# Splitting the weights of a two-layer decoder trunk: the low halves on one engine, in one instruction a unit

## The chip, the cores and the metric

The kernel runs on one core of a Trainium2 chip. The metric is the time of one execution on the device in microseconds (us), the median of three. Engines are named as in the profile: PE is TensorE (matrix products), PEld its weight loads, DVE is VectorE, ACT is ScalarE, POOL is GpSimd, SP is SyncE, which issues the DMAs. The products with the weights take fp32r operands, each split into a high and a low part.

## What is computed

Two layers of a decoder on 256 tokens of width 1024, each of them a token mixer, a cross-attention into 256 memory tokens and a SwiGLU feed-forward block (FFN), all added to the residual stream.

```python
# layer 0: combined projection, sparse attention A beside block attention B, one output projection
aq, ak, av, iq, ik, iw, bq, bk, bv = split(rms_norm(x) @ ab_w_in)
x += concat(dsa(aq, ak, av, iq, ik, iw), moba(bq, bk, bv)) @ ab_w_out
# layer 1: compressed, selected and window branches, mixed by gates
q, kc, vc, ks, vs, kw, vw, gt = split(rms_norm(x) @ nsa_w_in)
x += nsa(q, rope(q), compress(kc), compress(vc), ks, vs, kw, vw, sigmoid(gt)) @ nsa_w_out
# both layers
x += attention(rms_norm(x) @ w_q, rms_norm(mem) @ w_kv) @ w_o
g, u = split(rms_norm(x) @ ffn_w_in);  x += (silu(g) * u) @ ffn_w_out
```

## The kernel before

**The weight stream.** All weights pass through once as 232 units of two blocks of 128 rows and up to 512 columns (512 KB). A unit lands by DMA in one of three places named raw. `pusher` (line 384) makes its high part (`move`, ACT or DVE, one instruction on 128x1024) and then its low part, raw minus high, in two instructions, one for each block of rows (`tt`, line 313: DVE or POOL). Both parts lie in one of six places named whl. Then the raw place is free and the DMA of the unit three further on is issued. PE reads a unit for both tiles of 128 tokens: for each block the products high*high, high*low and low*high (`mm3`), twelve in all, most of them 512 columns wide.

**The order.** Nobody writes the order out by hand. Each piece of work is a generator that yields instructions; `Steps.run` (line 107) takes, again and again, the one that can start first by a rough clock (`Est`, line 140: a time for each engine, and for each tile's last write and reads). An instruction that two engines can do (`either`) goes to the one that is done with it first (`Op.best`, line 66); DVE has to be ahead by 0.4 us for that. So the costs written in `Est.Engine.cost` settle which engine does what and how instructions stand in each engine's queue. On the chip each engine works through its queue in that order; semaphores make it wait for operands.

**The work beside the stream.** Each projection's result is taken out of PSUM by DVE or ACT, normed, rotated (`rope`, four instructions on DVE or POOL), scaled, split and transposed by PE. Attention: scores (PE, tile sp), mask and maximum (DVE, sn<-sp), exponential (ACT), reciprocal (DVE), scaling (`scale`: sn<-sn,rc, DVE or POOL), transposes (PE, DVE or ACT to pt), values (PE, po). POOL alone makes the roots (`pow_half`, e.g. rq<-hss). In the FFN, DVE multiplies each result of u with silu(g) (t<-mm), PE transposes it, and DVE and ACT split it (slab<-tp).

**Main** (line 1468) walks through mixer, memory keys (mk), output projection (out), memory attention (mq, mv, mo) and FFN of each layer. `mixer1` ends with the projections q0 and q1; `mem_prep(1)`, which loads the memory tokens, transposes and splits them, is spawned ahead of these two, at line 1224. Its tiles are read by the products mk.

Of the kernel before, what the change touches and what calls it, by code (L numbers as in the profile page):

```python
# [8 lines left out]
F32 = mybir.dt.float32  # L9
# [6 lines left out]
P = 128  # L16
# [41 lines left out]
class Op:  # L58
    """an instruction to be issued, on the one of its engines that is done with it first"""
# [6 lines left out]
    def best(self):  # L66
        """(end, start, way)"""
        if self.deps is None:
            self.deps = [self.est.after(e, outs, ins) for e, outs, ins, _, _ in self.ways]
        r = []  # L70
        for d, w in zip(self.deps, self.ways):
            t = max(d, self.est.clk[w[0]])
            r.append((t + w[3], t, w))
        return min(r, key=lambda q: q[0] + (SHY if q[2][0] == "V" else 0.0))
# [9 lines left out]
class Steps:  # L84
    """The order of issue: pieces of work as generators, which yield instructions and conditions to wait for. Of the
    instructions that an engine could start next, one of the lowest rank goes first."""
# [9 lines left out]
    def go(self, th):  # L96
        """th up to its next instruction or to a condition that isn't met"""
# [42 lines left out]
class Est:  # L140
    """A rough clock of every engine and of every tile's last write, to emit work about when its operands are there."""

    def __init__(self, nc):
        self.clk = {"PE": 0.0, "V": 0.0, "S": 0.0, "G": 0.0, "D": 0.0}
# [11 lines left out]
    def when(self, ap, tab, e="", raw=True):  # L156
        """when engine e can go on after the uses of ap in tab; raw: it reads what they wrote"""
# [7 lines left out]
    def follow(self, old, new):  # L165
        """a new tile in the place of an old one is written after the old one's last use"""
# [18 lines left out]

    def issue(self, e, outs, ins, cost):
        t = max(self.clk[e], self.after(e, outs, ins))
# [9 lines left out]
        self.clk[e] = t  # L197
        for a in ins:
            self.note(a, self.rd, t, e)
# [52 lines left out]
class Slots:  # L252
    """n places of one size; a tile is placed in a free one"""
# [5 lines left out]
    def idle(self, i):  # L259
        """when the last use of place i ends"""  # L260
        return self.est.end(self.last[i]) if i in self.last else 0.0
# [22 lines left out]
def trunk(ctx: ExitStack, tc: tile.TileContext, I, out):  # L284
# [17 lines left out]
    def move(o, i, scale=None):  # L302
        """o = i * scale"""
# [4 lines left out]
    def together(ops):  # L308
        """ops one right after the other"""
# [3 lines left out]
    def tt(o, a, b, op):  # L313
        """o = a op b, all in SBUF"""
        return either(V.tensor_tensor(o, a, b, op=op), PO.tensor_tensor(o, a, b, op=op))

    def scale(s, r, n, m):
        """s [P, n*m] times r [P, n], in place"""
# [20 lines left out]
    # ---------------------------------------------------------------- loads of the small things  # L339
# [10 lines left out]
    # ---------------------------------------------------------------- weight stream  # L350
# [33 lines left out]
    def pusher():  # L384
        for i in range(len(plan)):
# [5 lines left out]
            for j in range(2):  # L391
                yield tt(u.lo[:, j], raw[:, j, :n], u.hi[:, j].bitcast(F32), OP.subtract)
# [37 lines left out]
    # ---------------------------------------------------------------- constants  # L430
# [34 lines left out]
    # masks of scores of the wrong sign: +1e30 where a key is not to be seen  # L465
# [10 lines left out]
    def tables():  # L476
# [24 lines left out]
        # products of the gains of queries and keys: dsa, moba, sel, win (these of the wrong sign), cmp, mem 0, mem 1  # L501
# [36 lines left out]
    def rope(q, H, a, b, half):  # L538
        """in place on the first 2*half dims of q [P, H, *]; a, b [P, 2, half]"""
# [9 lines left out]
    # ---------------------------------------------------------------- products with the weights  # L549
# [11 lines left out]
    def gemm(key, t, h, K, ev, need=None, part=None):  # L561
        """a pass of tile t: h(k) -> (hi, lo) [P, P], of which need tells; ev(psum, free, t) goes on with the result;
        part: the columns, where it isn't all"""
# [18 lines left out]
    # ---------------------------------------------------------------- norms and transposes  # L582
# [6 lines left out]
    def ms_root(ss, n, L, t):  # L589
        """mean square + eps and its root's inverse"""  # L590
# [7 lines left out]
    def evac_gain(ps, free, hi, lo, gain):  # L598
        """hi, lo [P, 4, P] of the product of ps with the gains [P, 4] of its blocks"""
# [9 lines left out]
    def norm(key, t, col, ver):  # L609
        """hT[t] from x[t], once both halves of x[t] are at version ver"""  # L610
# [14 lines left out]
    def root(key, t):  # L625
        """mean square + eps of the norm and its root's inverse"""
# [11 lines left out]
    def inv_rms(ps, H, dh, v, mul, add_k, r):  # L638
        """r [P, H] = (sumsq * mul + add_k * eps * v)^-0.5 of the heads of ps [P, H*dh]"""
# [10 lines left out]
    def stack_T(q, dst):  # L650
        """dst(i) [P, 4, P] of 4 heads: rows 0-63 hi, rows 64-127 lo, of the transposed heads of q [P, 8, HD]"""
# [12 lines left out]
    def keys_T(src, n, dst, gain):  # L664
        """dst(i) = (hi, lo) [P, P], both halves alike, of the transposed src(i) [P, 128] (a head twice) times gain;
        dst takes pairs at once"""
# [14 lines left out]
    # ---------------------------------------------------------------- softmax attention  # L681
    def scores(t, sp, spf, items, mask, gate, sn, snf, pv, fin):
        """items: (columns of sp, r) - softmax of the negated scores sp times r, times gate; pv(p) adds its transposed
        blocks p times the values"""
# [40 lines left out]
    def split(ps, free, hi, lo):  # L725
        """hi, lo of ps"""
# [4 lines left out]
    def finish(po, pof, t, half):  # L731
        """the transposed parts of the heads' outputs po for the output projection"""
# [6 lines left out]
    # ---------------------------------------------------------------- layer 0 mixer  # L739
# [203 lines left out]
    # ---------------------------------------------------------------- layer 1 mixer  # L943
# [19 lines left out]
    def mixer1():  # L963
# [30 lines left out]
        def compress():  # L994
# [40 lines left out]
            # the values of 8 heads, one below the other, each in its own columns  # L1035
# [490 lines left out]
```

## Time and profile before

| | us |
|---|---|
| runs: median (lowest to highest of 3) | 823.25 (822.81 to 828.13) |
| the profiled execution: span of its records | 824.0 |
| PE busy in it | 773.2 (94%) |
| DVE busy | 529.9 (64%) |
| POOL busy | 450.1 (55%) |
| ACT busy | 423.5 (51%) |

Busy is the time in which an instruction of the engine is on record as running, so an instruction that has started and is held up inside counts as busy. Idle time of an engine is put down to what ended it. In rows, whl<-raw,whl is a low part, whl<-raw a high part, and mm<-whl,h a product with the weights.

### The profile page before, as it was taken

To read this page: it belongs to the slowest core of one execution; us is meant where nothing else is said; L and a number is where in the kernel's file an instruction comes from. 1 tells how busy PE (TensorE), PEld (TensorE's weight loads), DVE (VectorE), ACT (ScalarE), POOL (GpSimd) and SP (SyncE) were. 2 spreads that over 40 slices of the span, in tenths; PEclk is the share of its full clock that TensorE was granted. 3 is DMA by queue.
4 is the path that set the end of the run, shared out by engine and by line. 5 is a ranking of instruction groups with operands and counts; after the bars stand their busy time and mean duration, and the time that the engine had idled before them with its cause. 6 is when DMAs were issued, how large, how long until landed. Compare 5 with 4: busy or idle time off the path is not lost.

```text
span 824.0 us, 12365 instructions
## 1 busy us (share of the span) xinstructions
PE 773.2 (94%) x4259; PEld 632.2 (77%) x4259; DVE 529.9 (64%) x1175; ACT 423.5 (51%) x799; POOL 450.1 (55%) x362
## 2 busy tenths in 40 slices
PE   5888999999999999999898988999999999999998
PEld 3676777797877878887677776778797778879886
DVE  6999998776655554322628889896867654454222
ACT  4566765465534433434425757665666344434441
POOL 4668844536555544667427765433536555545662
PEclk9899999999999999999999999999999999999999
DMA  6634423645565564886524732123535655645661
GB/s 188 179 103 112 155 92 103 180 127 154 153 181 160 176 187 115 214 228 205 152 64 124 219 112 78 45 61 103 151 99 160 202 162 160 191 140 164 209 206 73
DMA packets 69486, 121.31 MB, mean 147 GB/s; under 512 B 8420, under 2 KB 15664, under 8 KB 69424
## 3 DMA queue, kind: packets, MB, share of 16 engines
q1 hardware_dynamic: 69392, 120.53, 48.9%
q8 instruction: 33, 0.54, 0.3%
q14 instruction: 29, 0.24, 0.1%
q0 software_dynamic: 32, 0.00, 0.0%
HBM read 119.46 MB, written 1.05 MB: 146 GB/s over the span
## 4 chain that ended last, share of the span: by engine, by line
PE 56%; DVE 23%; DMA 7%; issue 6%; ACT 4%; POOL 3%; SPq 1%; ACTq 0%; DVEq 0%; POOLq 0%
PE mm L221 41%; PE po L221 8%; DVE whl L221 7%; PE tp L221 5%; DMA raw<-in_ffn_w_out 4%; ACT whl L221 3%; DVE t L221 3%; DVE sn L221 2%; POOL whl L221 2%; PE sp L221 2%; DVE slab L221 2%; DVE acc L221 2%; DMA raw<-in_ffn_w_in 2%; DMA raw<-in_nsa_w_in 1%; DVE x L221 1%
## 5 line engine op out<-in xcount | busy, mean ns | idle before, releaser
L221 POOL TENSOR_TENSOR whl<-raw,whl 128x512 fp32r<-128x512 f32 (+3 forms) x225 | 346.5, 1549 | 248.2 <-ACT whl L221 191.3
L221 PE MATMUL mm<-whl,h 128*128 128x512 f32 (+3 forms) x1776 | 403.7, 381 | 3.3 <-DVE whl L221 2.3
L221 PEld LDWEIGHTS mm<-whl,h 128*128 128x128 f32 x1776 | 311.8, 190 | 61.0 <-issue 2.8
L221 DVE TENSOR_TENSOR whl<-raw,whl 128x512 fp32r<-128x512 f32 (+3 forms) x239 | 216.2, 914 | 174.0 <-ACT whl L221 173.1
L221 ACT ACTIVATE whl<-raw 128x1024 fp32r<-128x1024 f32 (+3 forms) x203 | 204.8, 1011 | 182.4 <-DMA raw<-in_ffn_w_out 61.7
L221 PE MATMUL mm<-whl,slab 128*128 128x512 f32 (+1 forms) x840 | 201.4, 377 | 1.1 <-DVE x L221 1.1
L221 PEld LDWEIGHTS mm<-whl,slab 128*128 128x128 f32 x840 | 141.5, 189 | 27.4 <-issue 2.2
L221 PE MATMUL po<-whl,slab 128*128 128x512 f32 x264 | 68.4, 397 | 0.0
L221 PEld LDWEIGHTS po<-whl,slab 128*128 128x128 f32 x264 | 49.9, 190 | 11.9
L221 ACT ACTIVATE slab<-tp 128x256 fp32r<-128x256 f32 (+2 forms) x64 | 28.9, 472 | 47.2 <-PE tp L221 44.9
L221 ACT ACTIVATE sn<-sn,mx 128x128 f32<-128x128 f32 (+1 forms) x96 | 42.7, 447 | 10.1 <-DVE mx L221 9.3
L221 PE MATMUL tp<-ident,t 128*128 128x128 f32 x224 | 35.3, 278 | 10.7 <-DVE t L221 10.0
L221 PEld LDWEIGHTS tp<-ident,t 128*128 128x128 f32 x224 | 26.3, 142 | 21.3 <-DVE t L221 12.5
L221 POOL TENSOR_TENSOR sn<-sn,rc 128x512 f32<-128x512 f32 (+2 forms) x25 | 23.3, 932 | 34.4 <-DVE rc L221 19.4
L221 PE MATMUL tp<-ident,sn 128*128 128x128 f32 (+1 forms) x180 | 30.2, 280 | 6.3 <-DVE sn L221 2.9
L221 DVE CUSTOM_DVE_ANT_0 sn<-sp,cm,rq 128x128 f32<-128x128 f32 (+1 forms) x80 | 30.7, 407 | 5.8 <-PE sp L221 5.8
L221 ACT ACTIVATE pt<-tp 128x512 f32<-128x512 f32 (+2 forms) x49 | 25.8, 534 | 16.6 <-PE tp L221 15.8
L221 DVE CAST whl<-raw 128x1024 fp32r<-128x1024 f32 (+2 forms) x29 | 23.1, 795 | 15.3 <-PE mm L221 13.1
L221 DVE TENSOR_TENSOR x<-mm,x 128x512 f32<-128x512 f32 x36 | 24.5, 685 | 13.0 <-PE mm L221 13.0
L221 ACT ACTIVATE t<-mm,rh 128x512 f32<-128x512 f32 (+1 forms) x26 | 17.0, 655 | 30.4 <-PE mm L221 30.4
L221 PEld LDWEIGHTS tp<-ident,sn 128*128 128x128 f32 (+1 forms) x180 | 20.4, 140 | 14.2 <-issue 5.1
L221 ACT ACTIVATE h<-gv 128x512 fp32r<-128x512 f32 x20 | 12.6, 632 | 33.7 <-DVE gv L221 33.7
(208 smaller groups left out, 711.7 us busy)
## 6 DMA issues: line engine op xcount, KB each, us to landing
raw<-in_ffn_w_in SPq DMA_DIRECT2D x80, 512.0 KB, 4.3
raw<-in_ffn_w_out SPq DMA_DIRECT2D x44, 512.0 KB, 4.6
raw<-in_ab_w_in SPq DMA_DIRECT2D x16, 512.0 KB, 3.6
raw<-in_mem_w_kv SPq DMA_DIRECT2D x16, 512.0 KB, 3.7
raw<-in_nsa_w_in SPq DMA_DIRECT2D x16, 512.0 KB, 4.1
raw<-in_ab_w_out SPq DMA_DIRECT2D x8, 512.0 KB, 3.7
raw<-in_mem_w_q SPq DMA_DIRECT2D x8, 512.0 KB, 3.7
raw<-in_mem_w_o SPq DMA_DIRECT2D x8, 512.0 KB, 4.4
```

The costliest lines, as they stand in the source:

```text
L221: return f(*a, **{q: v() if q in ("start", "stop") and callable(v) else v for q, v in k.items()})
```

## The change

Four things are changed. The low part of a unit is one instruction on 128x1024, on DVE alone. `Est` gets one more clock, "port", which DVE instructions with two tensor inputs outside PSUM and all POOL instructions share: each starts, by the rough clock, not before the other's last one has ended. `Op.best` counts it when it picks the engine. And `mem_prep(1)` is spawned after q0 and q1, behind a new condition at which main stops until all queries of layer 1 have been prepared. Comments and blank lines, which the change removes too, are left out here.

```diff
@@ Op.best
-            t = max(d, self.est.clk[w[0]])
+            t = max(d, self.est.clk[w[0]], self.est.clk["port"] if self.est.locks(w[0], w[1], w[2]) else 0.0)
@@ Est
-        self.clk = {"PE": 0.0, "V": 0.0, "S": 0.0, "G": 0.0, "D": 0.0}
+        self.clk = {"PE": 0.0, "V": 0.0, "S": 0.0, "G": 0.0, "D": 0.0, "port": 0.0}
...
+    @staticmethod
+    def locks(e, outs, ins):
+
+        if e == "V":
+            big = [a for a in ins if a.shape[1:] != [1] and tuple(a.shape[1:]) != (1,)]
+            return len(big) > 1 and not any("PSUM" in str(a.space) for a in (*big, *outs))
+        return e == "G"
+
     def issue(self, e, outs, ins, cost):
-        t = max(self.clk[e], self.after(e, outs, ins))
+        lock = self.locks(e, outs, ins)
+        t = max(self.clk[e], self.after(e, outs, ins), self.clk["port"] if lock else 0.0)
...
+        if lock:
+            self.clk["port"] = t
@@ pusher
-            for j in range(2):
-                yield tt(u.lo[:, j], raw[:, j, :n], u.hi[:, j].bitcast(F32), OP.subtract)
+            yield V.tensor_tensor(u.lo, raw[:, :, :n], u.hi.bitcast(F32), op=OP.subtract)
@@ mixer1
-        spawn(mem_prep(1), 2)
         yield from both((1, "q0"), h, KD, ev_q(0))
         yield from both((1, "q1"), h, KD, ev_q(1))
+        yield lambda: len(qrT) == 2 * G and len(quT) == 2 * NT
+        spawn(mem_prep(1), 2)
```

What this does to the queues is seen at three places.

The first is POOL's queue at the start of the program. whl are the low parts, h the split of the normed input, rh and rk roots. Before:

```order
L221 TENSOR_TENSOR whl_120<-raw_79,whl_120 128x424
L221 TENSOR_TENSOR whl_162<-raw_81,whl_162 128x424
L221 TENSOR_TENSOR h_112<-gv_157,h_111 128x512
L221 TENSOR_TENSOR whl_174<-raw_85,whl_174 128x424
L221 TENSOR_TENSOR rh_190<-vh_189,mhalf 128x1
L221 TENSOR_TENSOR whl_217<-raw_160,whl_217 128x424
L221 TENSOR_TENSOR whl_240<-raw_172,whl_240 128x512
```

With the change, POOL's queue at the same place:

```order
L232 TENSOR_TENSOR rh_186<-vh_185,mhalf 128x1
L232 TENSOR_TENSOR rh_248<-vh_247,mhalf 128x1
L232 TENSOR_TENSOR rk<-ssk,mhalf 128x1 x2
L232 AFFINE_SELECT cm<-cm 128x128
L232 AFFINE_SELECT cmn<-cmn 128x30
L232 TENSOR_TENSOR rope_411<-t_241,ia 128x64
L232 TENSOR_TENSOR rope_411<-t_241,ib 128x8x4 x2
```

No low part is left on POOL (225 instructions in the whole program); the rope instructions, most of which DVE had, are there instead. POOL has 197 instructions in all, 367 before; DVE 1082, before 1161; ACT 671, before 654; PE has the same 3969.

The second is DVE's queue in the FFN of layer 0, between the products u of the two tiles: t<-mm takes such a result out of PSUM, slab<-tp splits the transposed one. Before:

```order
L221 SCALAR_TENSOR_TENSOR t_2628<-mm_2668,rh_2410,t_2628 128x512
L221 CAST whl_2722<-raw_2659 128x1024
L221 TENSOR_TENSOR slab_2709<-tp_2712,slab_2708 128x2x128
L221 TENSOR_TENSOR slab_2711<-tp_2712,slab_2710 128x2x128
L221 TENSOR_TENSOR whl_2722<-raw_2659,whl_2722 128x512
L221 TENSOR_TENSOR whl_2739<-raw_2673,whl_2739 128x512
L221 TENSOR_TENSOR whl_2751<-raw_2695,whl_2751 128x512
L221 SCALAR_TENSOR_TENSOR t_2669<-mm_2705,rh_2443,t_2669 128x512
```

With the change:

```order
L232 SCALAR_TENSOR_TENSOR t_2570<-mm_2608,rh_2359,t_2570 128x512
L232 CAST whl_2660<-raw_2599 128x1024
L232 TENSOR_TENSOR slab_2647<-tp_2650,slab_2646 128x2x128
L232 TENSOR_TENSOR slab_2649<-tp_2650,slab_2648 128x2x128
L232 TENSOR_TENSOR whl_2660<-raw_2599,whl_2660 128x1024
L232 TENSOR_TENSOR whl_2676<-raw_2612,whl_2676 128x1024
L232 TENSOR_TENSOR whl_2687<-raw_2632,whl_2687 128x1024
L232 SCALAR_TENSOR_TENSOR t_2609<-mm_2643,rh_2402,t_2609 128x512
```

The queue keeps its shape; the three low halves in it become three whole low parts.

The third is PE's queue in layer 1, at the end of the last product of q1 (mm<-whl,h). The products mk read a slab; tp, sp and po are attention's. Before:

```order
L221 MATMUL mm_4766<-whl_4593,h_113 128x512 x2
L221 MATMUL mm_4766<-whl_4593,h_114 128x512
L221 MATMUL mm_4998<-whl_4627,slab_4568 128x512
L221 MATMUL tp_4984<-ident,sn_4839 128x128 x4
L221 MATMUL tp_4994<-identr,t_4977 128x128 x4
L221 MATMUL mm_4998<-whl_4627,slab_4568 128x512
```

With the change:

```order
L232 MATMUL mm_4524<-whl_4459,h_113 128x512 x2
L232 MATMUL mm_4524<-whl_4459,h_114 128x512
L232 MATMUL tp_4661<-ident,sn_4565 128x128 x4
L232 MATMUL sp_4612<-slab_4144,slab_4556 128x256
L232 MATMUL sp_4612<-slab_4148,slab_4556 128x256
```

Before, the products mk follow at once and are mixed with attention's; with the change the next 80 rows of the queue are attention's alone, and mk begins behind them.

## Rows read from the trace of the kernel before

**Rows 1.** The page, part 1: busy time, share of span, instructions; PE, PEld.

```profile
PE 773.2 (94%) x4259; PEld 632.2 (77%) x4259; DVE 529.9 (64%) x1175; ACT 423.5 (51%) x799; POOL 450.1 (55%) x362
```

**Rows 2.** Busy time by stretch: start:end and length, then busy (instructions) by engine.

```profile
core 0: us, PE busy (x) PEld busy (x) DVE busy (x) ACT busy (x) POOL busy (x), PEclk, DMA share, GB/s
0.00:140.00 140.00, 118.06 (x651) 92.10 (x652) 126.89 (x380) 87.98 (x196) 89.49 (x91) 0.98 0.45 137
360.00:380.00 20.00, 20.00 (x88) 16.02 (x87) 6.28 (x9) 8.80 (x9) 14.69 (x9) 1.00 0.67 209
480.00:560.00 80.00, 75.26 (x604) 60.77 (x603) 73.70 (x269) 58.09 (x186) 34.86 (x40) 1.00 0.19 62
```

**Rows 3.** Groups by shape, low halves: busy us, mean ns | idle before.

```profile
L221 POOL TENSOR_TENSOR whl<-raw,whl 128x512 fp32r<-128x512 f32 x202 | 323.3, 1609 | 215.7 <-ACT whl L221 173.6 <-DVE whl L221 25.8 <-issue 4.7
...
L221 DVE TENSOR_TENSOR whl<-raw,whl 128x512 fp32r<-128x512 f32 x206 | 196.5, 963 | 162.7 <-ACT whl L221 161.9
```

**Rows 4.** Timeline at 24 us, POOL and DVE: start, us, engine, instruction.

```profile
23.75 3.05 POOL L221 TENSOR_TENSOR whl<-raw,whl 128x512 fp32r<-128x512 f32 x2 [0.16 <-ACT whl L221]
...
24.50 1.08 DVE L221 COPY ia<-cos 128x8 f32<-128x8 f32 x1
25.49 0.16 DVE L221 COPY ib<-nsin 128x8 f32<-128x8 f32 x1
25.57 1.27 DVE L221 COPY ia<-cos 128x8 f32<-128x8 f32 x1
```

**Rows 5.** Groups by shape: DVE splits with one input in PSUM; rope.

```profile
L221 DVE TENSOR_TENSOR slab<-tp,slab 128x256 fp32r<-128x256 f32 x44 | 17.4, 418 | 6.5 <-ACT slab L221 6.5
...
L221 DVE TENSOR_TENSOR slab<-tp,slab 128x512 fp32r<-128x512 f32 x4 | 2.7, 684 | 0.0
...
L221 DVE TENSOR_TENSOR rope<-t,rb 128x64 f32<-128x64 f32 x15 | 2.9, 212 | 0.0
```

**Rows 6.** Timeline of DVE: the two scalings on 128x1024 in SBUF.

```profile
61.31 2.31 DVE L221 TENSOR_TENSOR t<-t,rk 128x1024 f32<-128x1024 f32 x1
...
73.97 1.29 DVE L221 TENSOR_TENSOR t<-t,rk 128x1024 f32<-128x1024 f32 x1
```

**Rows 7.** Timeline of DVE: first and last held instruction of mixer 0.

```profile
9.09 1.49 DVE L221 TENSOR_TENSOR whl<-raw,whl 128x424 fp32r<-128x424 f32 x1
...
130.45 1.78 DVE L221 TENSOR_TENSOR sn<-sn,rc 128x512 f32<-128x512 f32 x1
```

**Rows 8.** Timeline of DVE: first and last held one of attention in layer 1.

```profile
495.11 1.08 DVE L221 TENSOR_TENSOR rope<-t,ra 128x128 f32<-128x128 f32 x1
...
562.17 1.77 DVE L221 TENSOR_TENSOR whl<-raw,whl 128x512 fp32r<-128x512 f32 x1
```

**Rows 9.** Timeline of PE: last values of attention 0 and 1, last product out.

```profile
134.04 0.66 PE L221 MATMUL po<-pt,bv 128*64 128x128 f32 x8
...
565.55 0.66 PE L221 MATMUL po<-pt,vv 128*64 128x128 f32 x8
...
579.76 1.64 PE L221 MATMUL mm<-whl,slab 128*128 128x512 f32 x6
```

**Rows 10.** Timeline of the FFN, from 249 us, and PE's last such wait.

```profile
249.01 4.80 DVE L221 TENSOR_TENSOR whl<-raw,whl 128x512 fp32r<-128x512 f32 x3
...
250.57 1.06 ACT L221 ACTIVATE whl<-raw 128x1024 fp32r<-128x1024 f32 x1 [0.39 <-DMA raw<-in_ffn_w_in]
253.74 0.74 DVE L221 SCALAR_TENSOR_TENSOR t<-mm,rh,t 128x512 f32<-128x512 f32 x1
...
254.53 0.66 PE L221 MATMUL tp<-ident,t 128*128 128x128 f32 x4 [1.15 <-DVE t L221]
...
725.23 0.66 PE L221 MATMUL tp<-ident,t 128*128 128x128 f32 x4 [1.15 <-DVE t L221]
```

**Rows 11.** Timeline at 89 us: a root on POOL, and DVE meanwhile.

```profile
88.92 0.68 DVE L221 TENSOR_TENSOR whl<-raw,whl 128x512 fp32r<-128x512 f32 x1
88.96 2.43 POOL L221 TENSOR_TENSOR rq<-hss,mhalf 128x8 f32<-128x8 f32 x1
...
90.68 0.67 DVE L221 CAST whl<-raw 128x1024 fp32r<-128x1024 f32 x1
```

## The prediction

> **What bounds the kernel now.** I read the page's busy times first, then the table by stretch, then the groups by shape, then timelines. PE is busy 94% [rows 1], which looks like a kernel with nothing to give. The table by stretch says otherwise. In the FFN, at 360 to 380 us, PE is busy all the time and gets 88 products through, 0.227 us each; DVE is busy a third of it [rows 2]. There PE is the bound. In mixer 0 (0 to 140 us) and attention of layer 1 (480 to 560 us) DVE is busy 126.9 of 140 and 73.7 of 80 us, and PE's instructions there, many of them small, stand further apart than their size needs [rows 2]. In these two stretches the end is set by DVE.
>
> But DVE's busy time is not all work. At 24 us two copies of 8 columns take 1.08 and 1.27 us, and one of the same size between them 0.16; the long ones end when POOL's two low halves end (23.75 + 3.05 = 26.80, against 25.57 + 1.27 = 26.84) [rows 4]. DVE stands still inside an instruction while POOL works in SBUF. The low halves show it from both sides: 0.963 us on DVE, 1.609 on POOL [rows 3], where a split of that width that has an input in PSUM takes 0.684 [rows 5].
>
> The Trainium skill (Perfetto Trace Analysis, Identifying the Most-Contended Engine) says that occupancy is a fair measure for VectorE of how near it is to its limit. Here the copies contradict it: seven eighths of their occupancy is standing still. By the page the mixers have no room for more work on DVE, and the sum would be that of the second rival below, 836; by the rows it is the one that follows.
>
> **The price of a whole low part.** From 256 to 512 columns a split goes from 0.418 to 0.684 us [rows 5], 1.04 ns a column, so 1024 columns take 0.684 + 512 x 0.00104 = 1.22 us. The bounds are the two scalings on 128x1024 from SBUF, 1.29 us and, held by POOL, 2.31 [rows 6]. I take 1.22, since POOL's low parts, which hold most, are gone.
>
> **Mixer 0.** I went through DVE's timeline to 134 us, where the last values of attention 0 are read [rows 9], and compared each instruction with the shortest of its form: 21 are held by a low half on POOL by over 0.3 us, 18.6 us in all [rows 7]. That goes. What comes is in the order: up to DVE's last score of this attention, 22 low halves at 0.69 (15.2 us) become 28 whole low parts at 1.22 (34.2), so +19.0. What leaves DVE up to there, mostly 36 pieces of rope (like the one at 0.21 us [rows 5]), three high parts and three copies of pt, comes to 9.6 us at the undisturbed duration of each form. Sum for DVE: -18.6 + 19.0 - 9.6 = -9. Attention ends 9 us sooner, and the order has 336 of the 384 weight products up to the end of out behind it by then, 296 before: 40 x 0.23 = 9 us less for PE to do afterwards. If PE had the room, mixer 0 would end 18 us sooner; but it must then be much denser than before, and the first 20 us wait for loads. Bounds 0 and -18; I take **-10**, the DVE sum and a little.
>
> **Layer 1, mixer.** From 480 us to the end of attention at 566 [rows 9] only five instructions are held by low halves, 4.7 us [rows 8]; the scalings of sn, which stay on POOL, hold about as much. Between the first and the last score DVE's own work falls by 3.4 us (order, undisturbed durations: fewer rope pieces, casts and splits of the memory, which come later, against 7 whole low parts for 10 halves). So attention gets shorter by some 8 us. The moved `mem_prep(1)` takes part of it back. It issues two loads on SP later, and main waits at the new condition for all queries; behind main wait mk and out. PE has 119 weight products inside attention before and 90 now, and 69 instead of 56 left at its end: 13 x 0.23 = +3.0 us. Ahead of 480 us the stretch is a chain of norms and projections, in which DVE is held some 9 us by low halves; I count -1 for it, since DVE is seldom what is late there. Sum **-6**; bounds +3 (nothing gained but the tail paid) and -12.
>
> **FFN.** The queue keeps its shape. At 249 us DVE needs 4.80 us for three low halves, and t<-mm behind them starts at 253.74; PE's transposes wait 1.15 us for it [rows 10]. Now: the first whole part from 249.1 to 250.3, the second to 251.5, the third after its high part on ACT (250.57 + 1.06 = 251.63) from 251.75 to 252.97. So t<-mm starts 0.77 us sooner, and 0.4 us of PE's wait stay. There are five of these in both FFNs, the last at 725 us [rows 10]: 5 x 0.77 = **-4**. Bounds: -5.7, or +2 if the third part is held by something. Everywhere else in the FFN, PE is full and hides what happens to DVE and POOL: a unit lasts PE 12 x 0.23 = 2.8 us, DVE 1.22.
>
> **At nothing.** The eight more high parts on ACT (1.06 us each [rows 10]) lie under PE, as ACT is half idle [rows 1]. Rope on POOL is slower for its own chain, but POOL loses 225 low halves of its 450 us. The raw places come free about 0.5 us sooner; PE waits hardly ever for a unit, so this gives nothing. The norms between blocks (140 to 220 and 560 to 640 us) are chains in which a held DVE instruction and a longer low part weigh about the same: 0, bounds 2 either way.
>
> **Sum.** -10 - 6 - 4 = -20 on a span of 824.0: 804.0. The median of the runs is 0.75 under the span, so **803** us.
>
> **Rivals.** *PE is the bound after all.* It is busy 94% [rows 1]; what DVE saves it spends waiting for PE, and only the FFN's waits go: 824.0 - 4 - 0.75 = 819. For it: 75.3 of 80 us of PE in attention are busy [rows 2]. Against it: there are 7.5 instructions a microsecond in that stretch, most of them on 64 to 256 columns, and a product of 512 columns alone takes 0.227. The Trainium skill (same page and section) calls matmul busy time a bad measure and weight loads a good one; by these, attention at 60.8 of 80 (76%) is nearly as full as the FFN at 16.0 of 20 (80%) [rows 2], which would speak for this rival. I hold against it that a load for a transpose takes as long as one for 512 columns, so that the share says little here. Chance 0.20.
>
> *DVE's busy time is work.* The waits do not go but change sides: a low part of 1.22 us meets POOL's scalings and ropes with twice the length. The clock "port" that should keep them apart is off in two ways: it leaves out instructions with one input, which are held too [rows 4], and counts the roots, during which DVE ran a low half in 0.68 and a high part in 0.67 us [rows 11]. Then mixer 0 grows by 19.0 - 9.6 = 9.4 us and the tail of layer 1 by 3: 824.0 + 12.4 - 0.75 = 836. It decides against the change when less than 9.4 of the 18.6 us in mixer 0 go away. The Trainium skill (SBUF — State Buffer, SBUF: two separate sides) has the pair of ports held for a whole instruction by whoever starts first; the copies agree. Chance 0.11.
>
> *Both mixers take the whole gain.* Mixer 0 -18, layer 1 -12, FFN -5: 824.0 - 35 - 0.75 = 788. It needs PE at full density in mixer 0 from 20 us on. Chance 0.16.
>
> **How the numbers follow.** My forecast has 0.53, from 795 to 811. The range 788 to 825 leaves out half of the large gain and the slow rival. A measurement of this kernel tells about 1% from no change, 815 to 831 us being "the same". Faster: 0.53 + 0.16 and a little of the first rival, 0.72; the same 0.18; slower 0.10.
>
> **What would show it.** In the profile of the changed kernel: a mean of 1.2 to 1.3 us for whl<-raw,whl on 128x1024; POOL busy about 130 us; DVE busy still near 530 us, but with no copy of 8 columns over 0.3 us; the last values of attention 0 at about 125 us and out 0 done 10 us sooner; attention of layer 1 some 8 us shorter with a longer run of weight products behind it; PE's waits for t<-mm in the FFN at 0.4 us or gone. I am wrong if whole low parts take over 1.5 us, if attention 0 ends at 134 us as before, or if PE stands idle between q1 and mk.

## The result, and the profile after

The changed kernel takes 802.4 us (801.8 to 802.9 in 4 runs) against 824.5 (822.8 to 828.1 in 4 runs): ratio 0.9725, 95% interval 0.9701 to 0.975. The forecast of 803 was met. Its terms were not: two came out too large, one too small, and one, put at nothing, was worth 6.8 us; most of this cancelled. One run of lo_halves below took 1301.8 us at a granted clock of 0.67, and its ratio leaves that run out. The profiled execution has a span of 800.1 us, 23.9 less than before; the stages below are its.

The page's busy times after, which answer [rows 1]:

```profile
PE 766.0 (96%) x4259; PEld 632.1 (79%) x4259; DVE 537.5 (67%) x1096; ACT 435.4 (54%) x816; POOL 130.9 (16%) x192
```

DVE is busy 7.6 us longer than before, though it now makes all low parts; POOL loses 319 us. The low part, grouped by shape (busy, mean ns), against the two halves of [rows 3], and the timeline of DVE at the copies of 8 columns [rows 4]:

```profile
L232 DVE TENSOR_TENSOR whl<-raw,whl 128x1024 fp32r<-128x1024 f32 x204 | 249.8, 1226 | 105.2 <-ACT whl L232 101.1
```
```profile
27.67 0.16 DVE L232 COPY ia<-cos 128x8 f32<-128x8 f32 x1
27.74 0.17 DVE L232 COPY ib<-nsin 128x8 f32<-128x8 f32 x1
27.82 0.17 DVE L232 COPY ia<-cos 128x8 f32<-128x8 f32 x1
```

The price of 1.22 us was right, and the copies that took 1.08 and 1.27 us take 0.16 and 0.17. The table by stretch (us, then busy time and instructions of PE, PEld, DVE, ACT and POOL, granted clock, DMA share, GB/s), for the two stretches of [rows 2] in which DVE was nearly full:

```profile
0.00:140.00 140.00, 121.18 (x673) 95.64 (x674) 116.21 (x344) 97.30 (x208) 54.27 (x92) 0.99 0.45 140
480.00:560.00 80.00, 76.74 (x586) 62.07 (x587) 65.74 (x217) 55.62 (x157) 20.57 (x24) 1.00 0.22 74
```

DVE stands idle 23.8 of the first 140 us, where it stood idle 13.1. What PE waited for (us in total, times, longest), the first two rows of before and of after:

```profile
PE tp L221 <- DVE t L221: 12.3, 11, 1.9
PE tp L221 <- DVE x L221: 6.9, 8, 3.8
```
```profile
PE mm L232 <- DVE whl L232: 6.9, 9, 1.5
PE tp L232 <- DVE slab L232: 5.6, 5, 2.0
```

Of the transposes' waits for t 0.3 us are left, in one place, of those for x none.

PE's timeline after, at the places of [rows 9]:

```profile
138.86 0.66 PE L232 MATMUL po<-pt,bv 128*64 128x128 f32 x8
...
543.36 0.66 PE L232 MATMUL po<-pt,vv 128*64 128x128 f32 x8
...
559.90 1.64 PE L232 MATMUL mm<-whl,slab 128*128 128x512 f32 x6
```

Attention 0 ends later than before (138.9 us, before 134.0), not sooner.

For most kernels of this study I read from PE's timeline where the first product of each block starts (for the end of g and u: the last), and got the length of each stage (us; each of the one execution that was profiled):

| kernel | to FFN 0 | FFN 0: g and u | FFN 0: out | layer 1: mixer, mk, out | mq, mo | FFN 1 | span |
|---|---|---|---|---|---|---|---|
| before | 205.3 | 129.7 | 69.9 | 176.3 | 46.6 | 196.2 | 824.0 |
| changed | 199.2 | 126.2 | 63.1 | 172.9 | 46.8 | 191.9 | 800.1 |
| lo_alone | 200.7 | 126.2 | 64.2 | 167.2 | 45.3 | 191.6 | 795.2 |
| lo_move | 200.1 | 125.9 | 63.8 | 172.7 | 45.2 | 192.1 | 799.8 |
| port_move | 210.9 | 125.9 | 66.0 | 181.8 | 51.1 | 192.9 | 828.6 |
| lo_halves | 198.2 | 126.2 | 68.0 | 170.3 | 44.9 | 192.0 | 799.6 |
| after_pool | 229.6 | 138.6 | 66.3 | 187.7 | 55.0 | 204.5 | 881.7 |
| after_roots | 208.6 | 126.0 | 63.6 | 181.6 | 47.0 | 191.8 | 818.6 |
| prep_mid | 199.6 | 126.3 | 63.1 | 175.0 | 45.4 | 191.9 | 801.3 |
| mid_noport | 201.3 | 126.2 | 63.7 | 169.2 | 45.6 | 192.0 | 798.0 |
| before_4raw | 209.5 | 131.6 | 64.2 | 178.9 | 46.7 | 195.1 | 826.0 |

So the 23.9 us come from the first mixer and memory attention (-6.1), FFN 0 (-3.5 and -6.8), layer 1's mixer (-3.4, with +0.2 behind it) and FFN 1 (-4.3).

### The profile page after: what moved, and what is told of

Read it like the earlier page. It is cut to its first block, busy times and chain, and to the rows that moved or that the text cites. A ratio compares the mean times of both kernels' runs of the same rounds, so it can differ in the third digit from the quotient of the medians.

```text
span 800.1 us, 11833 instructions
## 1 busy us (share of the span) xinstructions
PE 766.0 (96%) x4259; PEld 632.1 (79%) x4259; DVE 537.5 (67%) x1096; ACT 435.4 (54%) x816; POOL 130.9 (16%) x192
## 4 chain that ended last, share of the span: by engine, by line
PE 83%; DVE 7%; ACT 4%; DMA 2%; issue 2%; POOL 1%; SPq 0%; POOLq 0%; ACTq 0%; DVEq 0%
PE mm L232 61%; PE po L232 12%; PE tp L232 7%; PE sp L232 3%; DVE whl L232 2%; DMA raw<-in_ab_w_in 1%; DMA raw<-in_ffn_w_in 1%; ACT sn L232 1%; ACT whl L232 1%; DVE slab L232 1%; DVE acc L232 1%; ACT slab L232 1%; DVE sn L232 1%; DVE t L232 1%; POOL sn L232 1%
## 5 line engine op out<-in xcount | busy, mean ns | idle before, releaser
L232 PE MATMUL mm<-whl,h 128*128 128x512 f32 (+3 forms) x1776 | 397.8, 379 | 8.5 <-DVE whl L232 6.9
L232 DVE TENSOR_TENSOR whl<-raw,whl 128x1024 fp32r<-128x1024 f32 (+3 forms) x232 | 270.9, 1170 | 116.6 <-ACT whl L232 112.4
L232 ACT ACTIVATE whl<-raw 128x1024 fp32r<-128x1024 f32 (+3 forms) x211 | 213.2, 1014 | 160.1 <-DMA raw<-in_ffn_w_in 38.4
L232 POOL TENSOR_TENSOR rh<-vh,mhalf 128x1 f32<-128x1 f32 x12 | 9.5, 794 | 293.6 <-DVE vh L232 283.1
L232 POOL TENSOR_TENSOR sn<-sn,rc 128x512 f32<-128x512 f32 (+2 forms) x27 | 25.5, 944 | 43.5 <-DVE rc L232 28.6
L232 ACT ACTIVATE t<-mm 128x512 f32<-128x512 f32 (+2 forms) x46 | 23.7, 553 | 10.0 <-PE mm L232 8.0
L232 DVE SCALAR_TENSOR_TENSOR t<-mm,rh,t 128x512 f32<-128x512 f32 (+1 forms) x24 | 16.9, 704 | 18.2 <-PE mm L232 18.2
```

The costliest lines, as they stand in the source:

```text
L232: return f(*a, **{q: v() if q in ("start", "stop") and callable(v) else v for q, v in k.items()})
```

## The experiments

Ratios are to runs of the kernel before on the same chip; the interval is 95%. Kernels that ran on different chips are compared with some reserve: the medians of the kernel before lie between 822.9 and 824.8 us on the four chips of the experiments. Theory A: what counts is that POOL's low halves no longer hold DVE inside its instructions. B: the order that the port's clock makes. C: raw places come free sooner, so the weight stream is earlier. D: one instruction in place of two.

### The low part alone (lo_alone)

```diff
@@ against the changed kernel
-            t = max(d, self.est.clk[w[0]], self.est.clk["port"] if self.est.locks(w[0], w[1], w[2]) else 0.0)
+            t = max(d, self.est.clk[w[0]])
...
-        lock = self.locks(e, outs, ins)
+        lock = False
@@ mixer1
+        spawn(mem_prep(1), 2)
         yield from both((1, "q0"), h, KD, ev_q(0))
         yield from both((1, "q1"), h, KD, ev_q(1))
-        yield lambda: len(qrT) == 2 * G and len(quT) == 2 * NT
-        spawn(mem_prep(1), 2)
```

> One part of the change alone: the low part is one instruction on VectorE; the clock for the port is left out of the planner, and the preparation of the memory stays where it was, ahead of q0 and q1. Theory A (what counts is that GpSimd's low halves no longer hold VectorE inside its instructions, and that raw places come free sooner): most of the gain of 22 us is here, 802 to 808 us, and the FFN of layer 0 is about 10 us shorter than before, as in the changed kernel. Theory B (the order made with the port's clock does it): no more than 4 us come from this alone, 819 to 824 us, with the FFN's stalls still smaller but the mixers as long as before. My guess is A, 806.

Measured: 797.0 us, ratio 0.9667 (0.9622 to 0.9711). The low part alone gives the whole gain and, on another chip, 5 us more than the whole change. B is out as the source of the gain.

### The low part and the move (lo_move)

```diff
@@ against the changed kernel: the port's clock is left out, the move stays
-            t = max(d, self.est.clk[w[0]], self.est.clk["port"] if self.est.locks(w[0], w[1], w[2]) else 0.0)
+            t = max(d, self.est.clk[w[0]])
...
-        lock = self.locks(e, outs, ins)
+        lock = False
```

> Two parts of the change: the low part in one instruction on VectorE, and the preparation of the memory of layer 1 behind q0 and q1; the clock for the port is left out. It differs from the changed kernel by that clock alone, and from the kernel with the low part alone by the move alone. Theory A: the clock is worth little, since with the low parts gone GpSimd has few instructions left that meet VectorE's: within 4 us of 802. Theory B: without the clock rope and the scalings go where they collide: 8 us or more slower than the changed kernel, 810 or over. For the move: if it gives TensorE work at the wrong place (it had none of the stream from 468 to 500 us in the changed kernel), this is slower than the low part alone by 2 to 4 us.

Measured: 799.9 us (799.6 to 801.5; lo_alone on the same chip 795.3 to 798.6), ratio 0.9706 (0.9663 to 0.9749). With the move in both, the clock changes nothing that these runs can tell. The move lengthens layer 1's mixer from 167.2 to 172.7 us. The table by stretch from 468 us, of the changed kernel, of lo_move and then of lo_alone, shows it:

```profile
468.00:500.00 32.00, 26.35 (x244) 21.62 (x242) 28.15 (x111) 27.33 (x86) 15.60 (x17) 0.95 0.30 100
```
```profile
468.00:500.00 32.00, 28.76 (x243) 23.56 (x239) 27.77 (x104) 24.18 (x76) 12.93 (x16) 0.89 0.31 100
```
```profile
468.00:500.00 32.00, 30.57 (x248) 24.65 (x247) 28.77 (x98) 25.06 (x77) 18.00 (x19) 1.00 0.21 67
```

With the move PE stands idle 5.6 and 3.2 us of the 32, against 1.4, and the granted clock is 0.95 and 0.89 on average, part of the stretch at the lower of its two levels, where lo_alone keeps the full one. Main waits behind q1 for all queries, so no product with weights stands in PE's queue until mk: from 467.7 to 500.0 us in the changed kernel, from 479.9 to 509.8 in lo_move. In lo_alone mk follows q1 at once, at 478.5.

### The other two parts (port_move)

```diff
@@ against the changed kernel
-            yield V.tensor_tensor(u.lo, raw[:, :, :n], u.hi.bitcast(F32), op=OP.subtract)
+            for j in range(2):
+                yield tt(u.lo[:, j], raw[:, j, :n], u.hi[:, j].bitcast(F32), OP.subtract)
```

> The other two parts of the change without the first: the clock for the port and the move of the memory's preparation, while the low part stays two halves, each on VectorE or GpSimd as the planner finds. Theory A: the planner now steers around collisions by its own clock, so some of the gain is there, but low halves on GpSimd still hold VectorE's instructions with one input, which its clock leaves out: 812 to 822 us. Theory B: nearly all is there, 802 to 808 us. If the clock makes the planner send more low halves to VectorE, its busy time shows it, and the time falls with GpSimd's share.

Measured: 829.7 us, ratio 1.0073 (1.0046 to 1.01): below both expectations. The groups of halves:

```profile
L232 DVE TENSOR_TENSOR whl<-raw,whl 128x512 fp32r<-128x512 f32 (+2 forms) x340 | 244.4, 752 | 119.1 <-ACT whl L232 117.0
...
L232 POOL TENSOR_TENSOR whl<-raw,whl 128x512 fp32r<-128x512 f32 (+3 forms) x124 | 149.7, 1217 | 343.7 <-ACT whl L232 179.5
```

The planner leaves 124 halves on POOL. DVE is held less (a half on 128x512 takes 0.754 us, not 0.963; the row has smaller forms among them), and the FFNs gain nearly as in the changed kernel; but the stages with the two attentions are 5.6 and 5.5 us longer than before, and mq and mo 4.5; why, no run takes apart. The clock and the move are no gain without the low part on DVE.

### A subtraction on POOL for each unit (after_pool)

```diff
@@ pusher, against the changed kernel (dum: a tile that nobody reads; small tiles: 56 places, not 96)
             yield V.tensor_tensor(u.lo, raw[:, :, :n], u.hi.bitcast(F32), op=OP.subtract)
+            nc.gpsimd.tensor_tensor(dum[:, :n], u.hi[:, 0].bitcast(F32), u.hi[:, 1].bitcast(F32), op=OP.subtract)
```

> The changed kernel with its order, and for each unit of weights one more instruction on GpSimd, a subtraction of the high part's two blocks on 128 x 512 into a tile that nobody reads: GpSimd is again busy in SBUF for about one low half a unit, without holding a raw place. (For its space the small tiles have 56 places instead of 96.) Theory A (collisions inside VectorE's instructions were the cost): 232 instructions of 1.6 us against 202 before; VectorE's instructions are held again by about what the low halves held them, and the time goes most of the way back, 815 to 825 us. Theory C (the raw places and the earlier stream, or the order, were what counted): under 6 us are lost, 803 to 808 us, though VectorE's short copies take over 1 us again.

### A root on POOL for each unit (after_roots)

```diff
@@ pusher, the same place
+            nc.gpsimd.tensor_tensor(dum[:, :8], u.hi[:, 0, :8].bitcast(F32), mhalf[:, :8], op=OP.pow)
```

> The changed kernel with one more GpSimd instruction for each unit, as in after_pool and at the same place, but a root of 8 columns instead of a subtraction of 512: by the changed kernel's trace a root of 128 x 8 takes 1.78 us, the subtraction took 1.80. Its result is not read. GpSimd is thus busy equally long, with the same waits on the high part, and only its traffic in SBUF is gone. Theory A (the subtractions hold VectorE's instructions through the memory port): hardly anything is lost, 802 to 810 us, VectorE's low part stays at 1.2 to 1.3 us. The rival (a busy GpSimd costs the time by itself, by its waits, its queue ahead of the scalings and ropes, or by holding the weights' places): close to the 883 us of after_pool, 860 or over.

Measured: after_pool 882.8 us, ratio 1.0702 (1.0646 to 1.0758); after_roots 823.9 us, 0.9991 (0.9971 to 1.001). Both miss their expectations in size, and the pair still answers the question, best in FFN 0, where POOL has next to nothing of its own to do. The table by stretch from the first product of g and u to the last, changed kernel, after_pool and after_roots:

```profile
199.20:325.40 126.20, 126.20 (x622) 105.78 (x621) 74.21 (x97) 57.19 (x80) 1.82 (x4) 1.00 0.55 171
```
```profile
229.60:368.20 138.60, 130.34 (x622) 107.82 (x621) 98.27 (x97) 57.74 (x81) 80.08 (x48) 0.98 0.54 155
```
```profile
208.60:334.60 126.00, 126.00 (x623) 105.55 (x622) 73.50 (x97) 56.60 (x80) 89.41 (x48) 1.00 0.55 171
```

And the groups by shape in these stretches, after_pool and then after_roots:

```profile
L232 DVE TENSOR_TENSOR whl<-raw,whl 128x1024 fp32r<-128x1024 f32 x38 | 68.1, 1817 | 20.2 <-ACT whl L232 19.7
...
L232 DVE TENSOR_TENSOR slab<-tp,slab 128x256 fp32r<-128x256 f32 x20 | 7.5, 418 | 0.2 <-ACT slab L232 0.2
...
L404 POOL TENSOR_TENSOR dum<-whl 128x512 bf16<-128x512 f32 x38 | 72.4, 1906 | 49.3 <-ACT whl L232 39.4 <-DVE whl L232 8.5
```
```profile
L232 DVE TENSOR_TENSOR whl<-raw,whl 128x1024 fp32r<-128x1024 f32 x38 | 46.3, 1223 | 24.2 <-ACT whl L232 22.8
...
L404 POOL TENSOR_TENSOR dum<-whl,mhalf 128x8 bf16<-128x8 f32 x46 | 91.0, 1978 | 34.6 <-ACT whl L232 20.0 <-DVE whl L232 12.2
```

With roots POOL is busy 89 us, and DVE's low part takes 1.223 us, as without them; the stretch keeps its 126 us. With subtractions POOL is busy 80 us, the low part takes 1.817, and the stretch is 12.4 us longer, of which PE stood idle 8.3. DVE's splits with one input in PSUM (slab<-tp) take 0.418 with the subtractions too, as in [rows 5]. So A holds at this place: not POOL's time holds DVE, but what POOL does in SBUF, and not where DVE has an input in PSUM. All 37 low parts that begin in this stretch of after_roots run beside a root, for 1.16 of their 1.22 us on average; of the 20 splits in that of after_pool 12 run beside a subtraction, and none of them takes longer than 0.43 us. The root differs from the subtraction in its operation and in its width, and which of the two sets DVE free, no run separates.

How the subtraction holds DVE is seen where one meets two low parts (after_pool):

```profile
238.13 1.23 DVE L232 TENSOR_TENSOR whl<-raw,whl 128x1024 fp32r<-128x1024 f32 x1
238.48 2.03 POOL L404 TENSOR_TENSOR dum<-whl 128x512 bf16<-128x512 f32 x1
240.11 1.49 DVE L232 TENSOR_TENSOR whl<-raw,whl 128x1024 fp32r<-128x1024 f32 x1 [0.75 <-ACT whl L232]
```

The subtraction starts 0.35 us into the first low part and ends 1.15 us after that one's end (240.51 against 239.36); the second low part, which starts while the subtraction runs, ends 1.09 us after its end (241.60). The pattern is the same in the whole program (overlaps under 0.06 us left out): 141 subtractions that begin during a low part on 128x1024 end 1.13 to 1.17 us behind it, and 113 such low parts that begin during a subtraction end 1.08 to 1.13 us behind it. The two take turns, and the one that starts second has nearly all of its own work left when the first is done.

The Trainium skill (SBUF — State Buffer, SBUF: two separate sides) says that a VectorE instruction with two SBUF inputs and a GpSimd instruction that reads SBUF exclude each other for a whole instruction; the trace agrees for the subtraction and shows nothing of it for the root, which takes 8 columns in 2 us.

In the mixers after_roots does lose: 9.4 us to FFN 0 and 8.7 in layer 1. DVE is held no more there than in the changed kernel (its instructions up to FFN 0 add up to 186.6 us, there to 186.8), but scalings, ropes and real roots stand behind the added ones in POOL's queue. That my expectation of after_roots left out. It is the likely cause and not shown to be the only one, for the small tiles have fewer places too, and no run has that alone. The expectation of after_pool took the low halves of the kernel before as its measure and forgot that DVE now also carries the whole low part, 1.22 us a unit, beside the waits.

### Two halves on VectorE (lo_halves)

```diff
@@ pusher, against lo_alone
-            yield V.tensor_tensor(u.lo, raw[:, :, :n], u.hi.bitcast(F32), op=OP.subtract)
+            for j in range(2):
+                yield V.tensor_tensor(u.lo[:, j], raw[:, j, :n], u.hi[:, j].bitcast(F32), op=OP.subtract)
```

> The kernel with the low part alone (lo_alone, 797 us), but with the low part as two halves on VectorE instead of one instruction: so of the change only that the low part is VectorE's alone. By the durations two halves cost 2 x 0.69 = 1.38 us against 1.22, 0.16 us a unit, 37 us of VectorE over 232 units, little of it on the path. Theory A (GpSimd's absence is what counts): 797 to 802 us. Theory D (the single instruction is what counts, for VectorE is the bound): 808 us or more.

Measured: 799.4 to 801.3 us in three runs, ratio 0.97 (0.9675 to 0.9726). Nearly all of the gain comes with the low halves gone from POOL; the single instruction gives the last 3 us or so (lo_alone: 795.3 to 798.6 us, on another chip; the ratios' intervals overlap), 4.4 in the spans. In the profile the net of it lies in one place, the output part of FFN 0: 68.0 us, 64.2 in lo_alone. Its first mixer is 2.5 us shorter than there, and layer 1's 3.1 longer.

### A fourth raw place (before_4raw, lo_4raw)

```diff
@@ before_4raw against the kernel before, lo_4raw against lo_alone
-RAWS, PAIRS = 3, 6
+RAWS, PAIRS = 4, 6
...
-NSLAB = 23
+NSLAB = 21
```

> The kernel before with a fourth raw place (and for its space 21 slabs instead of 23); nothing else is changed. It asks why the second half of the FFN of layer 0 became 6.8 us shorter (from its last product g/u to the first of layer 1: 69.9 us before, 63.1 after). Theory C (the stream there turns round in the raw places, landing 4.6, high part 1.1, low half on GpSimd 1.8 us, and reaches layer 1 late): with four places that stretch is 63 to 65 us. The rival (VectorE, held by the low halves, is late with the additions to x): it stays at 69 to 70. The whole time: 816 to 820 by C, 823 to 826 by the rival; the lost slabs can cost a few us in the mixers.

> lo_alone with a fourth raw place and 21 slabs, as before_4raw was to the kernel before, where the stretch from the last product g/u of layer 0 to the first of kc fell from 69.9 to 64.2 us. If the low part on VectorE already took away what the raw places cost there, the stretch stays at 63.5 to 65 us (64.2 in lo_alone), and the lost slabs decide: 797 to 802 us. If landing and high part still turn round in three places, it falls below 62, and the whole to 794 to 796.

With a fourth raw place and all 23 slabs (before_raws4) the tiles have no room in SBUF: one pool needs 42.2 KB a partition where 38.2 are left. So two slabs go.

Measured: before_4raw 825.4 us, ratio 1.0031 (1.0005 to 1.0056); lo_4raw 800.9 us, 0.9725 (0.9683 to 0.9766). For the stretch that was asked about, C is right: with a fourth place it takes 64.2 us instead of 69.9. The whole time, 816 to 820 by C, shows none of it. The gain is lost elsewhere, most of it up to FFN 0 (209.5 against 205.3) and in layer 1's mixer (178.9 against 176.3); that the two missing slabs cost this is likely, but not tested alone. In lo_4raw the stretch takes 63.5 us, 64.2 in lo_alone: the low part on DVE had taken away what the raw places cost.

The mechanism is in the timelines. The end of FFN 0 before:

```profile
391.33 1.06 ACT L221 ACTIVATE whl<-raw 128x1024 fp32r<-128x1024 f32 x1 [1.38 <-DMA raw<-in_nsa_w_in]
...
392.42 0.69 DVE L221 TENSOR_TENSOR whl<-raw,whl 128x512 fp32r<-128x512 f32 x1 [1.74 <-ACT whl L221]
...
393.03 0.68 DVE L221 TENSOR_TENSOR x<-mm,x 128x512 f32<-128x512 f32 x1
...
393.77 0.66 PE L221 MATMUL tp<-ident,x 128*128 128x128 f32 x4 [3.80 <-DVE x L221]
```

The addition to x waits on no input here: it stands in DVE's queue behind a low half, whose high part on ACT waited for its DMA. PE stands still for 3.80 us, and the clock of 391 to 404.9 us is 0.88 on average (the first row below). After:

```profile
377.29 1.22 DVE L232 TENSOR_TENSOR whl<-raw,whl 128x1024 fp32r<-128x1024 f32 x1 [1.13 <-ACT whl L232]
...
379.00 0.69 DVE L232 TENSOR_TENSOR x<-mm,x 128x512 f32<-128x512 f32 x1 [0.48 <-PE mm L232]
...
379.96 0.60 PE L232 MATMUL tp<-ident,x 128*128 128x128 f32 x4
```

Same order in the queue, but the unit is there in time, x is added as soon as PE has its product, and PE never stops. The tables by stretch, before and after:

```profile
391.00:404.90 13.90, 10.62 (x44) 8.12 (x45) 8.55 (x11) 6.61 (x10) 5.37 (x5) 0.88 0.46 142
```
```profile
325.40:388.50 63.10, 63.10 (x282) 51.09 (x280) 34.89 (x37) 28.10 (x32) 0.00 (x0) 1.00 0.77 213
```

ACT's waits for the DMAs of ffn_w_out in this stretch, in the kernel before, before_4raw, lo_alone and lo_halves:

```profile
ACT whl L221 <- DMA raw<-in_ffn_w_out: 29.3, 18, 3.3
```
```profile
ACT whl L221 <- DMA raw<-in_ffn_w_out: 13.7, 11, 3.6
```
```profile
ACT whl L232 <- DMA raw<-in_ffn_w_out: 18.5, 15, 3.4
```
```profile
ACT whl L232 <- DMA raw<-in_ffn_w_out: 30.4, 19, 3.4
```

They are long where the stretch is long (69.9 and 68.0 us) and short where it is short (64.2 and 64.2; in the changed kernel 20.5 us at 63.1, in lo_4raw 8.0 at 63.5). In lo_halves PE again waits for x once, 2.3 us.

### Where the memory is prepared (prep_mid, mid_noport, vw_noport)

```diff
@@ mixer1: prep_mid against the changed kernel; mid_noport against lo_alone (spawn moved down by one line)
         yield from both((1, "q0"), h, KD, ev_q(0))
+        spawn(mem_prep(1), 2)
         yield from both((1, "q1"), h, KD, ev_q(1))
-        yield lambda: len(qrT) == 2 * G and len(quT) == 2 * NT
-        spawn(mem_prep(1), 2)
@@ vw_noport against lo_alone
+        spawn(mem_prep(1), 2)
         yield from both((1, "vw"), h, KD, ev_vw)
-        spawn(mem_prep(1), 2)
```

> The changed kernel with the preparation of layer 1's memory between q0 and q1, without the condition behind q1, so the port's clock and the low part stay. From lo_alone and lo_move (797.0 and 799.9 us) the move costs 3 to 5 us, in layer 1: from the first product of kc to the first of mq, 167 us against 173. If the loss is TensorE without products of the stream from 468 to 500 us (the mk products come behind the condition), it goes away here: 167 to 169 us for that stretch and 796 to 799 us in all. If the port's clock is what lengthens attention, the stretch stays at 172 or more, and the time at 801 to 804.

> prep_mid without the clock for the port: the low part on VectorE in one instruction, and the memory's preparation between q0 and q1. With lo_alone (ahead of q0) and lo_move (behind q1) it gives all three places without that clock, and with prep_mid one place with and without it. From the first product of kc to the first of mq, layer 1's mixer lasted 167.2 us in lo_alone, 172.7 in lo_move, 172.9 in the changed kernel and 175.0 in prep_mid. If the port's clock is what costs there, this one is near lo_alone, 166 to 169 us, and 795 to 799 in all. If it is the place, it lies at 172 or more, and the time at 800 to 803.

> lo_alone with the memory's preparation one projection earlier, ahead of vw instead of q0; no port clock. Behind q1 layer 1's mixer (first product of kc to the first of mq) took 172.7 us, between q0 and q1 169.2, ahead of q0 167.2. If it pays to have the mk products ready early, this goes on: 165 to 167 us and 794 to 797 in all. If ahead of q0 was early enough, it stays at 167 to 168, or grows, since the preparation's transposes and splits then stand among the norms and the rope of the keys: 797 to 800.

Measured: prep_mid 803.0 us, ratio 0.9735 (0.9715 to 0.9755); mid_noport 798.4, 0.9691 (0.9653 to 0.9729); vw_noport 796.9, 0.9667 (0.9634 to 0.97). Layer 1's mixer without the port's clock: 167.9 us with the preparation ahead of vw, 167.2 ahead of q0, 169.2 between q0 and q1, 172.7 behind q1. Ahead of q0 is early enough. With the clock it is 175.0 between them (5.8 more) and 172.9 behind q1 (0.2 more), so clock and place don't add. The stretch before attention 1, mid_noport and then prep_mid:

```profile
425.00:462.00 37.00, 34.68 (x214) 30.17 (x213) 29.16 (x70) 27.12 (x55) 20.70 (x28) 1.00 0.70 209
```
```profile
425.00:462.00 37.00, 34.49 (x207) 29.59 (x205) 27.91 (x57) 25.55 (x51) 21.91 (x33) 1.00 0.66 196
```

With the clock POOL has 33 instructions there instead of 28 and DVE 57 instead of 70, and attention's first score comes 73.9 us after the first product of kc instead of 68.2. That the clock sends work to the slower engine in a chain that is late is my reading; no run takes that one choice alone, so it stays open.

### The clock in layer 0 alone (port_l0)

```diff
@@ Est.locks, against lo_alone, with the clock of the changed kernel (off is False at first)
+        if self.off:
+            return False
@@ mixer1
+        est.off = True
```

> A version that may beat both kernels: the low part in one instruction on VectorE, the port's clock in layer 0 alone, where the changed kernel ends its mixer 1.5 us before lo_alone (the first product of the FFN at 199.2 against 200.7 us), and layer 1 without the clock and with the memory's preparation ahead of q0 as in lo_alone. If stages add up: layer 0 as in the changed kernel, layer 1 as in lo_alone, 795 us by 797 - 1.5. If the order in layer 1 depends on where layer 0 left the planner's clocks, the two don't add and it is anywhere from 795 to 803.

Measured: 797.0 us, ratio 0.9677 (0.9646 to 0.9708), the same as lo_alone. Its first product of kc comes 0.8 us sooner (390.3 us), but the first score of attention 1 at 460.3 in both; from there the two run alike. The clock is worth nothing here.

The fastest versions are lo_alone, vw_noport and port_l0, all at 797 us, 0.7% below the changed kernel. The intervals of lo_alone and of the changed kernel just touch (0.9711 and 0.9701); that the move costs time rests on lo_move and lo_alone, which ran on one chip.

## Why the prediction was right, and where it was not

*DVE's busy time was largely waiting.* Right. The copies, the low part at 1.226 us and DVE's 10.7 us less in the first 140 us say so, and the pair of subtraction and root shows the cause. The rival in which the waits change sides (836) fell.

*Mixer 0, -10.* Measured -6.1, within its bounds. The step that failed is "Attention ends 9 us sooner". DVE's own sum was good (-9; its busy time fell by 10.7), but DVE then stands idle instead: 23.8 us. The order puts 40 more products ahead of attention's end, which PE has to fit in, and attention ends 4.8 us later. Attention 0 no sooner than 134 us was one of the prediction's signs of being wrong. It is the planner's new clock that puts these products there: in the four kernels with the new low part and no clock (lo_alone, lo_move, mid_noport, vw_noport) 300 products come ahead, and the last values at 132.0 to 133.2 us; in the three with it (changed, prep_mid, port_l0) 336, and the last values at 138.9 to 139.3. So by the low part alone attention ends 1 to 2 us sooner, not 9. What I called the further gain is what came: the products behind attention. From the last values to the last product of out it is 23.6 us before (134.0 to 157.6) and 12.9 after (138.9 to 151.8), 10.7 less.

*FFN, -4.* The mechanism was right, the size too small. Three low halves took 4.80 us and t<-mm started 4.73 us after the first [rows 10]; now (DVE's timeline, then PE's)

```profile
242.30 3.79 DVE L232 TENSOR_TENSOR whl<-raw,whl 128x1024 fp32r<-128x1024 f32 x3
246.01 0.75 DVE L232 SCALAR_TENSOR_TENSOR t<-mm,rh,t 128x512 f32<-128x512 f32 x1
```
```profile
247.24 0.60 PE L232 MATMUL tp<-ident,t 128*128 128x128 f32 x4
```

it starts 3.71 us after, so 1.02 sooner and not 0.77, and nothing is left of PE's wait of 1.15 us. All five waits are gone: 5.7 us; a sixth of 0.3 and slightly shorter products bring the parts g and u of both FFNs to -7.8.

*"The raw places come free about 0.5 us sooner; PE waits hardly ever for a unit, so this gives nothing."* This is the step that was wrong: the end of FFN 0 became 6.8 us shorter, and a fourth raw place alone gave 5.7 of it (before_4raw). PE indeed doesn't wait for a unit there. But DVE's queue does, and the addition to x stands in it behind a low half. I had looked at who reads a unit, not at who queues behind its maker.

*Layer 1, -6.* Measured -3.4 for its mixer, +0.2 behind it. The gain is -9.1 (lo_alone), what the move takes back 5.5; I had -9 and +3.0. The clause "if PE stands idle between q1 and mk" came true in part: 5.6 of 32 us. The tail itself came as priced: from the last values to the first mq 15.7 us before and 18.0 after, +2.3 for my +3.0. The idle time ahead of mk, and the lower clock in it, were not priced.

*The sum.* -10, -6 and -4 stand against -6.1, -3.2 and -14.6. The total of 20 against 23.9 is near because a missing term of 6.8 and one that was 3.8 too small stood against two that were too large by 3.9 and 2.8. That the time came within 1 us of 803 is luck. The 0.75 in it helped: it takes the median of three runs from the span of another execution, whereas each run here with both on record took 1.65 to 2.05 us more than its span (801.8 against 800.1). In those terms a span of 804.0 is a time of about 805.7.

*The rival "PE is the bound"* (819) fell with the measured 802.4. One argument against it was misread: a load for a transpose does not take as long as one for a weight product, but 0.14 us against 0.19 on average in the 80 us of [rows 2].

## What to carry to other kernels

Read an engine's busy time against the shortest instance of each form before you call it work: a cheap test is a copy of a few columns that takes a microsecond. When a maker of buffers gets faster, look at what stands behind it in its own queue, not only at who reads the buffer. And test the parts of a change alone: here one of three carried all of it, and the other two together cost some 5 us.

## What the runs showed of the hardware

A GpSimd root on 128x8 (2 us) beside VectorE's low part on two SBUF inputs left it at 1.223 us, a GpSimd subtraction on 128x512 (1.9 us) made it 1.817. I had expected the first from one place [rows 11]; the 46 roots in an FFN bear it out. The subtraction and the low part take turns for whole instructions: the one that starts second ends 1.08 to 1.17 us after the first.
